# Projections of q, k and v in a hybrid decoder layer: seven half products per pair of column blocks, with the sums of the activations read back from DRAM

## The chip, the cores and the metric

One core of a Trainium2 chip runs the whole layer. The metric is the device time of one execution in microseconds; smaller is better. The engines are called by the profile's names: PE (matmul), PEld (its weight load), DVE (vector), ACT (scalar), POOL (GpSimd) and SP, which issues the DMAs.

## What is computed

The reference is one layer on 1024 tokens with 16 meta tokens ahead of them (L = 1040), width 1024, all in float32:

```python
xn = rms_norm(h, mix_pre_g[l])
proj = xn @ w_in[l]                      # z, xbc, dt, q, k, v
y_ssd = ssd_mixer(z, xbc, dt_raw, ...)   # Mamba-2 scan over chunks of 128
y_sb = rms_norm(stick_breaking_attention(q, k, v)..., sb_norm_g[l])
mix = jnp.concatenate([y_ssd, y_sb], axis=-1) @ w_out[l]
h = h + rms_norm(mix, mix_post_g[l])
xn = rms_norm(h, ffn_pre_g[l])
gu = xn @ w_up[l]
g = causal_dwconv(gu[..., :D_FF], ffn_conv_w[l], ffn_conv_b[l])
f = (jax.nn.gelu(g, approximate=True) * gu[..., D_FF:]) @ w_down[l]
h = h + rms_norm(f, ffn_post_g[l])
```

Stick-breaking attention weights a key by a sigmoid of q·k and by the product of (1 - sigmoid) over the keys between it and the query. q, k and v are 1024 wide each: 8 pairs of heads, 128 columns per pair of heads.

## The kernel before, in words

The normed input is transposed into `xs` (128 rows of one eighth of the width, 8 eighths, 1040 tokens) and split into a rounded part and the rest, so that a float32 product becomes three matmuls in the fast format: high·high, high·low, low·high. A projection block has 128 columns of a weight; `load_w` (L146 to L154) loads it (0.52 MB into the tag `wraw`, two buffers), ACT rounds it (`whi`), POOL takes the rest (`wlo`), three buffers each. `project_steps` (L156 to L168) then runs 8 eighths x 3 matmuls for each of three chunks of tokens (400, 384 and 256 wide, `CH`), each into one of two PSUM buffers `mm`; ACT copies a chunk out, and for k DVE takes the rest (L388, L389).

The order of the program: norm and transposes; projections for the SSD group (x, z, B, C); the scan of group 0 with the projections of group 1 between its chunks; the scan of group 1 with the first projections of q, k and v between its chunks; then the attention, a loop over 8 pairs of heads p and 8 query blocks i (from L989). One turn of that loop holds, on PE: the scores `z` of block i (L765), `av` of an earlier block (L802), one or two steps of the generator `fill`, which are the projections of the next pair of heads (half a chunk each, 12 matmuls), the transposes `tw` of an earlier block (L787), and another step of `fill`. PE's order is thus written out by hand; the orders of DVE, ACT, POOL and SP come from the scheduler of the framework, and each engine works its list in order. SP issues every DMA, in its order too.

For one query block, ACT takes two sigmoids of z, DVE multiplies along the keys with a scan (L773), POOL multiplies weight and remainder (L775, L776), PE transposes, ACT copies. `split_q` (L737 to L743) rounds a q block on DVE (`qh`, L741) and takes the rest (`ql`, L742). After q, k and v of the last pair of heads, the output product of the SSD half (`ssd_half`) takes the place of `fill`. The FFN that follows (L1304) already uses a scheme of seven half products, with its x sums held in SBUF.

## Time and profile before

| | |
|---|---|
| runs of the kernel before | 1734.75 us median of 3 (1733.84 to 1738.6) |
| the profiled execution | 1735.83 us, its span 1733.7 us |
| granted PE clock, mean | 0.995 |
| q, k, v projections on PE | from 310.4 to 820.1 us, between other work |
| attention, first scores of p = 0 | 400.5 us |
| moved by DMA | 173.87 MB, mean 100 GB/s |

In a row of groups stand line, engine, operation, output<-inputs, shape and count, then busy time, mean ns of one, and the idle time ahead of them with what ended it. In a timeline row stand the start and the length in us; matmul lengths are pipelined, so the distance of two starts is what one costs. In a row of windows stand the busy time of each engine in that stretch, the granted clock, the mean share of the 16 DMA engines in use, and GB/s.

### The profile page before, as it was taken

To read this page: it belongs to the slowest core of one execution; us is meant where nothing else is said; L and a number is where in the kernel's file an instruction comes from. 1 tells how busy PE (TensorE), PEld (TensorE's weight loads), DVE (VectorE), ACT (ScalarE), POOL (GpSimd) and SP (SyncE) were. 2 spreads that over 40 slices of the span, in tenths; PEclk is the share of its full clock that TensorE was granted. 3 is DMA by queue.
4 is the path that set the end of the run, shared out by engine and by line. 5 is a ranking of instruction groups with operands and counts; after the bars stand their busy time and mean duration, and the time that the engine had idled before them with its cause. 6 is when DMAs were issued, how large, how long until landed. Compare 5 with 4: busy or idle time off the path is not lost. (4 is left out here: it accounts for less than half of the span.)

```text
span 1733.7 us, 28039 instructions
## 1 busy us (share of the span) xinstructions
PE 1708.7 (99%) x11230; PEld 1498.9 (86%) x11230; DVE 1114.4 (64%) x1230; ACT 821.6 (47%) x1370; POOL 858.3 (50%) x645
## 2 busy tenths in 40 slices
PE   7999999999999999999999999999999999999998
PEld 6999889888999998998687778999988888887886
DVE  5752964775676686668531457676666666758777
ACT  5423653545566566567553245433333333343544
POOL 4323663685566576555642124587766777400001
PEclk9999999999999999999999999999999999999999
DMA  4232343231011111112215544233332222395335
GB/s 163 58 113 97 101 130 104 67 104 38 26 38 37 38 31 33 38 50 86 82 50 172 175 165 136 63 117 96 110 100 92 92 91 92 114 330 188 104 112 180
DMA packets 90674, 173.87 MB, mean 100 GB/s; under 512 B 10704, under 2 KB 35816, under 8 KB 90544
## 3 DMA queue, kind: packets, MB, share of 16 engines
q1 hardware_dynamic: 90544, 172.08, 31.0%
q8 instruction: 88, 1.44, 0.3%
q14 instruction: 42, 0.34, 0.1%
HBM read 122.32 MB, written 49.73 MB: 99 GB/s over the span
## 5 line engine op out<-in xcount | busy, mean ns | idle before, releaser
L775 POOL TENSOR_TENSOR bt<-bt,kp 128x256 f32<-128x256 f32 (+7 forms) x128 | 213.2, 1684 | 184.5 <-DVE kp L773 147.7
L773 DVE TENSOR_TENSOR_SCAN kp<-kp,hold 128x272 f32<-128x272 f32 (+7 forms) x128 | 183.4, 1473 | 26.0 <-ACT kp L766 14.1
L1247 POOL TENSOR_TENSOR wlo<-wr,whi 128x1024 fp32r<-128x1024 f32 x43 | 106.2, 2479 | 38.0 <-ACT whi L1246 38.0
L1751 POOL TENSOR_TENSOR fms<-fms 128x1 f32<-128x1 f32 x8 | 2.7, 333 | 223.7 <-DMA ar<-fda 187.5
L766 ACT ACTIVATE kp<-z 128x288 f32<-128x288 f32 (+6 forms) x112 | 82.5, 737 | 52.2 <-PE z L765 27.9
L1246 ACT ACTIVATE whi<-wr 128x1024 fp32r<-128x1024 f32 x43 | 45.6, 1059 | 111.5 <-PE fX L1304 68.3
L165 PE MATMUL pj_v<-xs,wh_v 128*128 128x400 f32 (+2 forms) x384 | 94.9, 334 | 0.0
L1376 DVE SCALAR_TENSOR_TENSOR ga<-gr,pp,ga 128x1024 f32<-128x1024 f32 x44 | 72.3, 1643 | 34.9 <-ACT ga L1369 34.1
L165 PE MATMUL pj_k<-xs,wh_k 128*128 128x400 f32 (+2 forms) x384 | 94.4, 333 | 0.0
L789 ACT ACTIVATE th<-tw 128x1024 f32<-128x1024 f32 (+2 forms) x96 | 75.6, 816 | 38.5 <-PE tw L787 38.4
L165 PE MATMUL pj_q<-xs,wh_q 128*128 128x386 f32 (+2 forms) x384 | 93.8, 331 | 0.0
L165 PE MATMUL pj_X<-xs,wh_X 128*128 128x400 f32 (+2 forms) x384 | 93.1, 330 | 0.0
L1636 ACT ACTIVATE dh<-ar 128x512 fp32r<-128x512 f32 x77 | 48.5, 630 | 92.4 <-PE dnB L1714 44.7
L165 PE MATMUL pj_z<-xs,wh_z 128*128 128x386 f32 (+2 forms) x384 | 91.5, 326 | 0.0
L741 DVE CAST qh<-q 128x128 fp32r<-128x128 f32 x64 | 46.9, 734 | 67.1 <-PE z L765 66.7
L1637 DVE TENSOR_TENSOR dl<-ar,dh 128x512 fp32r<-128x512 f32 x77 | 53.2, 691 | 50.3 <-ACT dh L1636 47.5
L951 PE MATMUL mo<-woa,yh 128*128 128x512 f32 x256 | 85.2, 400 | 0.0
L767 ACT ACTIVATE bt<-z 128x288 f32<-128x288 f32 (+6 forms) x112 | 82.8, 740 | 0.0
L802 PE MATMUL av<-th,v 128*64 128x128 f32 x1152 | 78.1, 280 | 0.0
L787 PE MATMUL tw<-ident,bt 128*128 128x128 f32 x576 | 75.4, 274 | 0.0
L802 PEld LDWEIGHTS av<-th,v 128*64 128x64 f32 x1152 | 62.3, 138 | 14.0 <-issue 11.3
L787 PEld LDWEIGHTS tw<-ident,bt 128*128 128x128 f32 x576 | 65.5, 141 | 5.8 <-issue 2.7
(560 smaller groups left out, 5635.2 us busy)
## 6 DMA issues: line engine op xcount, KB each, us to landing
wr<-in_w_up SPq DMA_DIRECT2D x44, 512.0 KB
fds<-ga SPq DMA_DIRECT2D x44, 256.0 KB
b<-in_w_down SPq DMA_DIRECT2D x44, 256.0 KB
ar<-fds SPq DMA_DIRECT2D x44, 256.0 KB
fda<-ga SPq DMA_DIRECT2D x33, 256.0 KB
ar<-fda SPq DMA_DIRECT2D x33, 256.0 KB
yk<-yd SPq DMA_DIRECT2D x16, 512.0 KB
wor<-in_w_out SPq DMA_DIRECT2D x12, 512.0 KB
```

The source lines that it names most:

```text
L165: mm(acc[:ncol, :n - s], a[:, k, :ncol], xs[c0][:, b, k, s:n], start=(k == 0 and j == 0), stop=(k == KB - 1 and j == 2))
L766: nc.scalar.activation(kp[:, :, a:a + w], z[:, :, :w], AF.Sigmoid, scale=-QSCALE)
L767: nc.scalar.activation(bt[:, :, a:a + w], z[:, :, :w], AF.Sigmoid, scale=QSCALE)
L773: nc.vector.tensor_tensor_scan(kp[:, j][:, ::-1], kp[:, j][:, ::-1], hold[:, L - n:L][:, ::-1], 0.0, op0=ALU.mult, op1=ALU.max)
L775: nc.gpsimd.tensor_tensor(bt[:, j, 0:m], bt[:, j, 0:m], kp[:, j, 1:m + 1], op=ALU.mult)
L787: nc.tensor.transpose(tw[:, j, b, :], bt[:, j, c0:c0 + P], ident)
L789: nc.scalar.activation(th[:, :, :nb, :], tw[:, :, :nb, :], AF.Copy)
L802: mm(av[halves[j], :], v[:, kb, halves[j]], th[:, j, b, :], start=kb == 0, stop=kb == i)
L951: mm(acc, u[:, k, :], v[:, cs], start=(k == 0 and j == 0), stop=(k == 7 and j == 2))
L1247: nc.gpsimd.tensor_tensor(l, raw, h.bitcast(F32), op=ALU.subtract)
L1376: nc.vector.scalar_tensor_tensor(v, self.g[jj][:, :, i:i + 256], fconv_w[:, j, i:i + 1], v, op0=ALU.mult, op1=ALU.add)
L1637: sub(lo[:, k], raw, hi[:, k].bitcast(F32), op=ALU.subtract)
```

## The change

Two blocks of 128 weight columns form a pair: (k, q), (v, q), (k, v), twelve pairs in all. The contraction is cut in two halves (4 eighths each) and the tokens in two halves of 520. Of the eight half products of such a 2 x 2 scheme, Winograd's form needs seven, on sums of weight quarters (s1 to s4) and of x quarters (t1 to t4). A half product is done in two steps of 260 tokens: 4 eighths x 3 matmuls = 12 matmuls each, so a pair has 14 steps. They run in the order 1 (x quarter b11), 2 (b21), 6 (t2), 5 (t1), 3 (b22), 7 (t3), 4 (t4).

- The x sums are formed once, during the scan of group 0: per eighth on POOL and DVE, rounded by ACT, and written to DRAM (`xt13`, `xt42`, 16 DMAs).
- For the steps with t1 to t4, the sums are read back into a ring of two slots, which takes the place of the quarter of x that no product uses by itself. A slot holds one step: 128 rows x 4 eighths x 520 float32 = 1.065 MB. When a step has used its slot, the DMA for the unit after next is issued into it. There are 96 units.
- DVE forms the weight sums (4 of 512 elements per pair). ACT rounds and POOL splits three and a half weight tiles per pair, where two blocks took two.
- The results of products 1 and 2 are copied out by ACT (k: ACT and DVE), those of 6, 5, 3, 7 and 4 are added by DVE from PSUM to what is in SBUF.
- `qh` is rounded by ACT and no longer by DVE.
- Chunks of the other projections are 320, 400 and 320 wide; a few constants move into the SSD pool, the scratch of dt into a buffer of `rkl`, which gets a third buffer; `FILL` goes, and `fill` is now run in steps of 12 matmuls throughout, 3 per turn for i < 3 and 2 for the others.

The core of the diff:

```diff
-CH = [(0, 400), (400, 384), (784, 256)]
+CH = [(0, 320), (320, 400), (720, 320)]
+HT = L // 2
+HP = HT // 2
+QKV = [(1, "a11", "b11", True), (2, "a12", "b21", False), (6, "s2", "t2", True), (5, "s1", "t1", True),
+       (3, "s4", "b22", False), (7, "s3", "t3", True), (4, "a22", "t4", False)]
...
+    def x_sums(k):
+        r1, r2 = (rp.tile([P, 2, HT], F32R, tag="rkl", name=f"xr{j}_{k}", bufs=3).bitcast(F32) for j in range(2))
+        for r, kk in ((r1, k), (r2, k + 4)):
+            nc.gpsimd.tensor_tensor(r, xq[:, kk, :, 0].bitcast(F32), xq[:, kk, :, 1].bitcast(F32), op=ALU.add)
+        nc.gpsimd.tensor_tensor(r1[:, 0], r1[:, 1], r1[:, 0], op=ALU.subtract)
+        nc.gpsimd.tensor_tensor(r1[:, 1], r2[:, 1], r1[:, 1], op=ALU.subtract)
+        nc.vector.tensor_tensor(r2[:, 1], r2[:, 1], r1[:, 0], op=ALU.subtract)
+        nc.vector.tensor_tensor(r2[:, 0], r2[:, 0], r2[:, 1], op=ALU.subtract)
...
+    ring = [xq[:, 0:4, 1].rearrange("p k b n -> p k (b n)")[:, :, 2 * HP * s:2 * HP * s + 2 * HP] for s in range(2)]
+    units = [(n, c) for _ in range(12) for n in ("t2", "t1", "t3", "t4") for c in range(2)]
...
+    def load_unit():
+        u = loaded[0]
+        if u < len(units):
+            loaded[0] += 1
+            (src, j), c = t_of[units[u][0]], units[u][1]
+            nc.sync.dma_start(out=ring[u % 2].bitcast(F32), in_=src[:, j, c].rearrange("p k b n -> p k (b n)"))
...
+        def split(self, raw, n1, n2):
+            hi, lo = self.slot(n1)
+            nc.scalar.activation(hi, raw, AF.Copy)
+            nc.gpsimd.tensor_tensor(lo, raw, hi.bitcast(F32), op=ALU.subtract)
...
+        def sums(self):
+            r1, r2 = self.r
+            nc.vector.tensor_tensor(r1[:, 0:4], r1[:, 0:4], r2[:, 0:4], op=ALU.subtract)
+            nc.vector.tensor_tensor(r2[:, 0:4], r2[:, 0:4], r2[:, 4:8], op=ALU.add)
...
+        def step(self, s):
+            (n, wn, xn, first), c = QKV[s // 2], s % 2
...
+            for k in range(4):
+                for j, (w, b) in enumerate(((hi, 0), (hi, 1), (lo, 0))):
+                    mm(acc[:, :HP], w[:, k, :], rv[:, k, b, :], start=first and k == 0 and j == 0,
+                       stop=k == 3 and j == 2, skip_group_check=not first)
+            if xn[0] == "t":
+                load_unit()
...
+            elif n == 6:
+                add(c21, a, c21, op=ALU.add)
+            elif n == 5:
+                add(c22, a, c21, op=ALU.add)
...
+    def qkv_flow():
+        post = []
+        for n, b in enumerate(blocks):
...
+            for s in range(14):
+                b.step(s)
...
+                if s == 0:
+                    b.split_s34()
+                if s == 2 and nxt:
+                    nxt.load(0)
+                if s == 3:
+                    b.split_s1()
+                if s == 5 and nxt:
+                    nxt.load(1)
+                    nxt.split_a()
+                if s == 8 and nxt:
+                    nxt.sums()
...
+                if s == 11 and nxt:
+                    nxt.split_s2()
...
-        nc.vector.tensor_copy(qh, q)
+        nc.scalar.activation(qh, q, AF.Copy)
...
-            run(fill, 1 + (i < FILL[p]))
+            run(fill, 1 + (i < 3))
...
-            run(fill, int((p > 0 or i > 3) and (p, i) != (6, 6)))
+            run(fill, 1)
```

How the change moves instructions is seen best at two places. The first is SP's list in the attention of p = 4. Before, the only large loads there are the weight blocks (`wr_q`, `wr_k`, `wr_v`), beside the store of an attention result (`yd`):

```order
L150 DMA wr_q_5690<-in_w_q 128x1024
L826 DMA yd_101<-ysc_4269 128x8x128
L150 DMA wr_k_5923<-in_w_k 128x1024
L433 DMA mvd<-v_5203 16x128
L150 DMA wr_v_6193<-in_w_v 128x1024
```

Now, about pairs 7 to 9 (`wr_8`, `wr_9` are the weights of pairs 8 and 9, `xall<-xt_109` the units of t1 and t3, `xall<-xt_110` those of t4 and t2):

```order
L385 DMA wr_8_6847<-in_w_k 128x1024
L966 DMA yd_92<-ysc_6127 128x8x128
L376 DMA xall<-xt_109 128x4x520
L385 DMA wr_8_6986<-in_w_v 128x1024
L376 DMA xall<-xt_109 128x4x520 x3
L376 DMA xall<-xt_110 128x4x520
L522 DMA mvd<-v_7177 16x128
L376 DMA xall<-xt_110 128x4x520 x3
L385 DMA wr_9_7460<-in_w_k 128x1024
L385 DMA wr_9_7570<-in_w_q 128x1024
L376 DMA xall<-xt_109 128x4x520 x4
```

Eight ring loads now stand between the first weight load of pair 8 and those of pair 9, and the loads of t1 of pair 8 stand behind both weight loads of pair 9.

The second place is PE's list in pair 4, where product 6 (t2) ends and product 5 (t1) begins. Before, the same place in the attention (block i = 3 of a pair of heads, scores `z_3`) reads x from SBUF only:

```order
L787 MATMUL tw_0_0_4895<-ident,bt_0_4645 128x128 x2
L165 MATMUL pj_v_0_4900<-xs_133,wh_v_4740 128x400 x2
L165 MATMUL pj_v_0_4900<-xs_133,wl_v_4741 128x400
...
L811 MATMUL twc_4913<-ident,cb_4068 128x128 x2
L765 MATMUL z_3_0_4921<-kh_3782,qh_3_4854 128x264 x2
...
L802 MATMUL av_0_4948<-th_0_0_4898,v_4495 64x128 x2
L822 MATMUL avc_4953<-thc_4916,vc_3894 64x256 x2
L165 MATMUL pj_v_0_4900<-xs_133,wh_v_4740 128x400 x2
```

Now (`pj_4_0` and `pj_4_1` are the two steps of pair 4's product; `whis_4_5012` is the weight sum s2, so those are the steps with t2, and `whis_4_5230` is s1, so those are the steps with t1):

```order
L464 MATMUL pj_4_0_5272<-xall,wlos_4_5013 128x260
L464 MATMUL pj_4_1_5287<-xall,whis_4_5012 128x260 x2
...
L927 MATMUL tw_0_0_5308<-ident,bt_0_5029 128x128 x2
L464 MATMUL pj_4_0_5313<-xall,whis_4_5230 128x260 x2
...
L951 MATMUL twc_5328<-ident,cb_4348 128x128 x2
L905 MATMUL z_3_0_5336<-kh_4176,qh_3_5245 128x264 x2
...
L942 MATMUL av_0_5363<-th_0_0_5311,v_4560 64x128 x2
L962 MATMUL avc_5368<-thc_5331,vc_3952 64x256 x2
L464 MATMUL pj_4_1_5374<-xall,whis_4_5230 128x260 x2
```

The first row is the end of the first t2 step. The load of the first t1 unit goes into the slot that this step frees, and the first t1 step (the row after `tw`) needs it: between them stand one step and two transposes.

326 lines of the change are left out of this document (196 added, 130 removed).

## The prediction

> **What bounds the kernel now.** I begin with the span and the busy times on the page, then read the stretches of the attention, where the changed projections lie.
>
> ```profile
> span 1733.7 us, 28039 instructions
> PE 1708.7 (99%) x11230; PEld 1498.9 (86%) x11230; DVE 1114.4 (64%) x1230; ACT 821.6 (47%) x1370; POOL 858.3 (50%) x645
> PEclk9999999999999999999999999999999999999999
> ```
>
> PE is busy for 99% of the span at full clock, so a matmul taken away shortens the kernel, unless PE then waits. The windows of the attention say who could make it wait:
>
> ```profile
> core 0: us, PE busy (x) PEld busy (x) DVE busy (x) ACT busy (x) POOL busy (x), PEclk, DMA share, GB/s
> 500.00:560.00 60.00, 60.00 (x517) 54.37 (x516) 41.12 (x43) 37.46 (x64) 36.38 (x28) 1.00 0.13 36
> 560.00:620.00 60.00, 60.00 (x503) 54.68 (x501) 43.55 (x40) 35.47 (x62) 35.65 (x29) 1.00 0.13 36
> ```
>
> PE has no gap at all; DVE is at 70%, ACT and POOL at 60%, and the DMA engines are nearly free (0.13). The time is PE's work, and the question is what the change makes of it and which of the other four comes late.
>
> **PE's work.** One eighth of a projection chunk is three matmuls. The distance of the starts of two such triples is their price, for 400, 384, 256 and, from the FFN, 258 columns (13 matmuls between the last two rows):
>
> ```profile
> 205.79 0.53 PE L165 MATMUL pj_X<-xs,wh_X 128*128 128x400 f32 x2
> 206.34 0.53 PE L165 MATMUL pj_X<-xs,wh_X 128*128 128x400 f32 x2
> ...
> 212.35 0.51 PE L165 MATMUL pj_X<-xs,wh_X 128*128 128x384 f32 x2
> 212.87 0.51 PE L165 MATMUL pj_X<-xs,wh_X 128*128 128x384 f32 x2
> ...
> 200.09 0.40 PE L165 MATMUL pj_X<-xs,wh_X 128*128 128x256 f32 x2
> 200.45 0.40 PE L165 MATMUL pj_X<-xs,wh_X 128*128 128x256 f32 x2
> ```
>
> ```profile
> 1157.05 0.28 PE L1304 MATMUL fA<-b11l,whi 128*128 128x258 f32 x1
> 1158.61 0.28 PE L1304 MATMUL fA<-b11h,wlo 128*128 128x258 f32 x1
> ```
>
> That is 0.55, 0.52 and 0.36 us a triple, and 0.12 us a matmul of 258 columns. A block of k or v costs 8 x (0.55 + 0.52 + 0.36) = 11.4 us, one of q (386 columns first) 11.2; 24 blocks are 272 us. Afterwards there are 12 pairs x 14 steps x 4 triples = 672 triples of 260 columns at 0.363: 244 us. **PE saves 28 us.** The chunks of 320, 400 and 320 of the other projections hold as many columns as before: nothing.
>
> **The ring.** This is the new wait. A step with a t sum can start only when its 1.065 MB have landed, and the load can be issued only when the step two units earlier has freed the slot. What a load takes is shown by the first loads of the kernel, issued by SP and awaited by ACT, and by the stretch in which the DMA is busiest:
>
> ```profile
> 0.79 0.39 SPq L235 DMA_DIRECT2D xt<-in_meta  x1
> 1.24 0.41 SPq L235 DMA_DIRECT2D xt<-in_x  x1
> 1.70 0.42 SPq L143 DMA_DIRECT2D gpre<-in_rows  x1
> ```
>
> ```profile
> 2.88 1.05 ACT L263 ACTIVATE junk<-xt 16x1024 f32<-16x1024 f32 x1 [0.81 <-DMA xt<-in_meta]
> ...
> 5.02 1.06 ACT L263 ACTIVATE junk<-xt 128x1024 f32<-128x1024 f32 x1 [0.99 <-DMA xt<-in_x]
> ...
> 8.21 1.06 ACT L263 ACTIVATE junk<-xt 128x1024 f32<-128x1024 f32 x1 [2.04 <-DMA xt<-in_x]
> ```
>
> ```profile
> 1515.00:1560.00 45.00, 45.00 (x200) 37.23 (x199) 24.56 (x39) 20.26 (x36) 0.00 (x0) 1.00 0.95 328
> ```
>
> The 64 KB of meta, issued at 0.79, are there at 2.88: about 2.0 us are fixed. From 5.02 to 8.21 gpre and the next x block land, 1.05 MB in 3.2 us; the busiest stretch gives 328 GB/s at a share of 0.95, 345 at full. So a unit streams in 3.1 us and is there 5.1 us after its slot is free; two units issued one after the other are there after 5.1 and 8.2.
>
> Against this stands PE's work between the end of the first step of one t product and the steps of the next. Prices of the work between (distance of starts):
>
> ```profile
> 588.44 1.91 PE L787 MATMUL tw<-ident,bt 128*128 128x128 f32 x16
> 590.11 0.60 PE L165 MATMUL pj_k<-xs,wh_k 128*128 128x384 f32 x2
> ...
> 593.15 1.97 PE L802 MATMUL av<-th,v 128*64 128x128 f32 x32
> 595.05 0.62 PE L165 MATMUL pj_k<-xs,wh_k 128*128 128x384 f32 x2
> ```
>
> ```profile
> 599.21 0.40 PE L765 MATMUL z<-kh,qh 64*128 64x264 f32 x2
> ...
> 600.14 0.44 PE L802 MATMUL av<-th,v 128*64 128x128 f32 x4
> 600.41 0.60 PE L822 MATMUL avc<-thc,vc 128*64 128x256 f32 x4
> ```
>
> 16 transposes take 1.67 us, 32 matmuls of av 1.90, the six z matmuls of 264 columns 0.93, a step 1.45. In the place shown from PE's list (pair 4, t2 to t1) one step and two transposes, 1.45 + 0.3 = 1.8 us, stand ahead of the first t1 step, which needs 5.1: it waits 3.3. The second comes at 1.8 + 1.45 + 0.3 + 0.9 + 0.3 + 0.5 = 5.3, which with the wait is 8.6: no more. I priced all 47 passages from one t product to the next in this way. Those across products 1 and 2 or 3 have 7 to 20 us and wait once (1.6 us, pair 2). Of the 24 direct ones (t2 to t1, t3 to t4), where 2 to 4 steps and the attention work between come to 3.5 to 10 us, 17 wait, by 0.1 to 4.7 us, the worst in pair 2, where three steps follow each other. The sum is **32 us**. With 0.6 us more of fixed time it is 45; at 36 GB/s for a share of 0.13 (277 at full, 3.85 us a unit) 60; at 4.5 us for one and 7 for two, 17. I take 32.
>
> **The weight loads in SP's list.** Each pair loads two blocks of 0.52 MB, 1.5 us each at that rate, and from pair 3 on one or both stand ahead of the t1 loads. They wait until POOL has split the last weights in that buffer, and what stands behind them in SP's list waits along. Before, SP already waits there, with nothing urgent behind:
>
> ```profile
> SPq L150 <- POOL wl_v L152: 127.8, 7, 26.3
> ```
>
> ```profile
> L775 POOL TENSOR_TENSOR bt<-bt,kp 128x1024 f32<-128x1024 f32 x12 | 34.8, 2922 | 21.9 <-DVE kp L773 13.0 <-PE z L765 4.8 <-PE vtc L428 4.1
> ```
>
> The buffer of the second block is freed by the split that starts after step 3, one step ahead of the one that frees the ring slot. If POOL is prompt this costs nothing. If the split takes ACT 1.06 (1024 wide, as in the rows above) and POOL 2.44 (the row of `wl_v` below) behind one product of 2.92, it takes 6.4 in all, and less the 2.7 of a step with its share of attention (57.1 us below by 21 steps) 3.7 us, for some ten pairs: 37. I take 10, nearer to nothing, since most t1 loads then only queue behind 1.5 us of weights.
>
> **The engines.** One p takes 60.7 us now (score rows of two pairs of heads), and 1.5 pairs fall into it:
>
> ```profile
> 575.15 0.33 PE L765 MATMUL z<-kh,qh 64*128 64x144 f32 x2
> ...
> 635.81 0.34 PE L765 MATMUL z<-kh,qh 64*128 64x144 f32 x2
> ```
>
> ```profile
> L741 DVE CAST qh<-q 128x128 fp32r<-128x128 f32 x56 | 42.3, 754 | 56.4 <-PE z L765 56.1
> L389 DVE TENSOR_TENSOR kl<-pj_k,kh 128x256 fp32r<-128x256 f32 x7 | 2.9, 416 | 4.5 <-ACT kh L388 4.5
> L152 POOL TENSOR_TENSOR wl_v<-wr_v,wh_v 128x1024 fp32r<-128x1024 f32 x6 | 14.6, 2440 | 0.5 <-ACT wh_v L151 0.5
> L1641 DVE TENSOR_TENSOR b<-b,b 128x512 f32<-128x512 f32 x44 | 29.1, 685 | 0.0
> ```
>
> PE's share falls to 57.1 us. DVE, 43 us now, loses 8 casts (6.0), gains 15 additions from PSUM at 0.42 (6.3) and 6 weight sums at 0.69 (4.1): 47.5, or 83%. POOL gains 2.25 splits of 2.44 (5.5): 41, 72%. ACT gains 8 short casts and 2.25 roundings: about 69%. None becomes the bound by itself, but each step's PSUM buffer is needed two steps later, and now mostly DVE must empty it, between its scans. The nearest row is the FFN, which works like this: PE's idle time there is 3.3 us for DVE and 1.1 for POOL in 410 us.
>
> ```profile
>   DVE pu L1400: 3.3, 9
>   POOL wlo L1247: 1.1, 3
> ```
>
> With the scans between I take **8 us**; the ends are 0 (hidden in the ring's waits) and 40 (one us for every fourth step). The x sums put 8 additions of 1040 elements and 8 of 520 on POOL ahead of the attention, about 30 us at `wl_v`'s rate; POOL is idle for half of the span, and I price them at nothing behind PE's projections, at 8 us if a weight split comes late.
>
> DVE's price depends on POOL. The same `ql` takes 0.29 us or 1.99:
>
> ```profile
> 578.88 1.99 DVE L742 TENSOR_TENSOR ql<-q,qh 128x128 fp32r<-128x128 f32 x1
> ...
> 584.90 0.29 DVE L742 TENSOR_TENSOR ql<-q,qh 128x128 fp32r<-128x128 f32 x1
> ```
>
> The Trainium skill ("SBUF — State Buffer", Who interferes with whom) says that a DVE instruction with two SBUF inputs and a GpSimd instruction that reads SBUF block each other for a whole instruction, while one with a single SBUF input goes free. By it the additions from PSUM stay at 0.42, and the weight sums, two SBUF inputs each, are the part of this change that pays: held by 1.7 us each they would make DVE 57.7 us a p, as much as PE. The trace agrees as far as `ql` goes.
>
> **The sum.** 1735.8 - 28 + 32 + 10 + 8 = 1757.8 in the profiled execution, which lies 1.1 above the median: **1757 us**, 1.3% slower.
>
> **The rivals.**
> - *The ring is hidden, and the kernel is faster.* If a unit takes 4.5 us and two take 7, the waits are 17 us and the rest hides in them: 1735.8 - 28 + 17 = 1725, 1724 as a median. It decides at 28 us of waiting in all. For it: the DMA engines are 87% free in the attention. Against: no row here streams faster than 345 GB/s, and a cover of 1.8 us is too short for any load. Chance 0.2. The Trainium skill ("DMA: Bandwidth & Descriptors", Anatomy of one DMA) gives 2.0 us plus bytes at 436 GB/s, 4.4 us for a unit, and is the page for this rival; the trace agrees with its 2.0 and not with its rate.
> - *Gain and waits cancel.* 32 us of ring waits with all else inside them, less what PE's own small pauses add to the cover: within 5 us of 1735. Chance 0.13.
> - *SP and DVE make it far worse.* SP held by POOL (37) and DVE late (18): 1735.8 - 28 + 32 + 37 + 18 = 1795. For it: SP's waits on POOL above, and DVE at 83%. Against: while PE waits, they catch up. Chance 0.17.
> - *The half products don't save what they count.* If each of 168 steps starts 0.2 us late, 34 us are lost and the result is near 1780 with the ring. Against: a chunk's first triple at 590.11 is the usual one after transposes, and the program before has nearly as many starts. Chance 0.05.
>
> **How the numbers follow.** The forecast (1741 to 1780) has the remaining 0.45. The range leaves out the lower part of the first rival and the worst of the third: 1722 to 1797. Less than 0.3%, about 5 us, is what a measurement of this kernel can't tell from no change. Faster: 0.2. Same: 0.13. Slower: 0.67.
>
> **What would show it.** The triples of the new products should start 0.36 us apart. In the list of waits PE should wait for DMA into `xall` some 20 times, longest near 5 us, in the steps of t1 and t4 and not of t2 and t3; SP's waits for POOL should stand ahead of t1 loads. DVE should be over 80% busy from 400 us on. I am wrong if a unit lands in under 4.5 us, or if PE's longest waits are for DVE or POOL.

## The result, and the profile after

The changed kernel takes **1864.91 us** (median of 4 runs, 1854.08 to 1872.54) against 1734.89 us of the kernel before (4 runs, 1733.84 to 1738.6): a ratio of 1.074, 95% interval 1.068 to 1.080. The forecast was 1757, the range ended at 1797. The profiled execution took 1872.54 us.

The page of the changed kernel, its span, busy times and clock:

```profile
span 1870.8 us, 29199 instructions
PE 1734.4 (93%) x11518; PEld 1512.9 (81%) x11518; DVE 1219.8 (65%) x1360; ACT 853.2 (46%) x1460; POOL 959.2 (51%) x685
PEclk9989999998899999989989999999999999999999
```

PE is now idle for 136 us where it was idle for 25. And it is busy for 26 us *more*, although its matmuls should take 28 less: the clock row has eights where every digit was a nine. The windows of the three stages (ahead of the first q/k/v step; from there to the first matmul of the output product; the rest) say where. Before:

```profile
0.00:310.40 310.40, 299.73 (x1943) 280.34 (x1943) 182.95 (x203) 140.23 (x265) 133.21 (x119) 0.99 0.35 109
310.40:833.40 523.00, 519.34 (x4237) 462.42 (x4236) 369.44 (x406) 317.12 (x565) 328.72 (x270) 1.00 0.17 49
833.40:1733.70 900.30, 889.59 (x5056) 756.10 (x5054) 562.03 (x623) 364.25 (x541) 396.37 (x257) 0.99 0.39 127
```

After:

```profile
0.00:333.80 333.80, 306.91 (x1942) 285.23 (x1943) 212.70 (x226) 147.30 (x275) 170.05 (x135) 0.97 0.40 124
333.80:968.40 634.60, 537.12 (x4526) 471.60 (x4525) 441.75 (x519) 343.08 (x645) 397.16 (x298) 0.92 0.61 203
968.40:1870.80 902.40, 890.34 (x5055) 756.02 (x5053) 565.33 (x616) 362.79 (x541) 392.01 (x252) 0.99 0.38 127
```

The first column is the length; behind it stand the busy times of PE, PEld, DVE, ACT and POOL, the granted clock, the share of the DMA engines in use, and GB/s. The first stage lost 23.4 us, the second 111.6, the rest 2.1. In the second, idle time went from 3.7 to 97.5 us (+94); busy time went from 519.3 to 537.1 where 28 less were due (491.3), so 46 us more were worked off at a lower clock: -28 + 94 + 46 = 112.

The list of PE's waits (in total, times, longest):

```profile
PE pj L464 <- DMA xall<-xt: 59.7, 22, 7.6
...
PE tt_X L611 <- DVE xtk L607: 9.7, 4, 4.8
PE pj L464 <- DVE kl L443: 8.8, 5, 2.6
```

The ring is the longest row, as forecast, but twice as long; about 38 us in the second stage are waits for other engines, in many short rows; and the `tt_X` row lies ahead of the attention, where the forecast had nothing.

A passage of the ring as the forecast described it, from the timeline of SP and then of PE (start, length, and in brackets the idle time ahead):

```profile
608.38 2.05 SPq L376 DMA_DIRECT2D xall<-xt  x2
610.07 0.36 SPq L376 DMA_DIRECT2D xall<-xt  x1
...
613.41 0.51 PE L464 MATMUL pj<-xall,whis 128*128 128x260 f32 x2 [1.43 <-DMA xall<-xt]
613.88 0.40 PE L464 MATMUL pj<-xall,whis 128*128 128x260 f32 x2
614.24 0.41 PE L464 MATMUL pj<-xall,whis 128*128 128x260 f32 x2
...
618.55 0.79 PE L464 MATMUL pj<-xall,whis 128*128 128x260 f32 x2 [2.98 <-DMA xall<-xt]
619.35 0.64 PE L464 MATMUL pj<-xall,whis 128*128 128x260 f32 x2
620.00 0.64 PE L464 MATMUL pj<-xall,whis 128*128 128x260 f32 x2
```

The first row holds both issues, the second row the later of them alone. The first unit is used 5.03 us after its issue (5.1 was forecast). The second is issued 1.7 us later, when its own slot comes free, and is used 8.5 us after that, 10.2 after the first's issue. The 8.2 of the forecast was for two loads issued right behind each other, so these 10.2 are not a slower load: SP issued 0.52 MB of an attention result (`yd`) at 612.52, and from 613.4 to 618.5 the DMA engines moved 335 GB/s, near the forecast's full rate of 345. The new triples start 0.36 us apart at 613.88, as forecast. But after the wait of 2.98 us they start 0.65 us apart (619.35 to 620.00), on the same tiles: PE works at about half its rate. Stretches like this are the eights in the clock row, and no term of the sum.

### The profile page after: what moved, and what is told of

Its sections match the earlier page's. It is cut to its first block, busy times and chain, and to the rows that moved or that the text cites. A ratio compares the mean times of both kernels' runs of the same rounds, so it can differ in the third digit from the quotient of the medians.

```text
span 1870.8 us, 29199 instructions
## 1 busy us (share of the span) xinstructions
PE 1734.4 (93%) x11518; PEld 1512.9 (81%) x11518; DVE 1219.8 (65%) x1360; ACT 853.2 (46%) x1460; POOL 959.2 (51%) x685
## 5 line engine op out<-in xcount | busy, mean ns | idle before, releaser
L464 PE MATMUL pj<-xall,whis 128*128 128x260 f32 x960 | 206.6, 313 | 76.2 <-DMA xall<-xt 59.7
L913 DVE TENSOR_TENSOR_SCAN kp<-kp,hold 128x272 f32<-128x272 f32 (+7 forms) x128 | 201.1, 1611 | 91.2 <-ACT kp L906 72.0
L464 PEld LDWEIGHTS pj<-xall,whis 128*128 128x128 f32 x960 | 162.3, 207 | 94.4 <-issue 29.2
L464 PE MATMUL pj<-xall,wlos 128*128 128x260 f32 x480 | 144.7, 301 | 2.3 <-POOL wlos L393 2.3
L464 PEld LDWEIGHTS pj<-xall,wlos 128*128 128x128 f32 x480 | 99.5, 207 | 2.8 <-POOL wlos L393 2.8
L160 PE MATMUL pj_z<-xall,wh_z 128*128 128x306 f32 (+2 forms) x384 | 94.4, 333 | 0.0
L160 PE MATMUL pj_X<-xall,wh_X 128*128 128x320 f32 (+1 forms) x384 | 94.0, 330 | 0.0
L1766 ACT ACTIVATE dh<-ar 128x512 fp32r<-128x512 f32 x77 | 48.5, 630 | 94.3 <-PE dnB L1844 44.8
L1084 PE MATMUL mo<-xall,yh 128*128 128x512 f32 x256 | 85.7, 402 | 0.0
L393 POOL TENSOR_TENSOR wlos<-wr,whis 128x1024 fp32r<-128x1024 f32 x24 | 64.2, 2677 | 39.4 <-ACT whis L392 36.3
L464 PE MATMUL pj<-xall,whia 128*128 128x260 f32 x384 | 76.2, 297 | 3.0 <-DVE q L489 3.0
```

The source lines that it names most:

```text
L160: mm(acc[:ncol, :n - s], a[:, k, :ncol], x_cols(k, b, c0 + s, n - s), start=(k == 0 and j == 0), stop=(k == KB - 1 and j == 2))
L464: mm(acc[:, :HP], w[:, k, :], rv[:, k, b, :], start=first and k == 0 and j == 0, stop=k == 3 and j == 2, skip_group_check=not first)
L913: nc.vector.tensor_tensor_scan(kp[:, j][:, ::-1], kp[:, j][:, ::-1], hold[:, L - n:L][:, ::-1], 0.0, op0=ALU.mult, op1=ALU.max)
L1084: mm(acc, u[:, k, :], v[:, cs], start=(k == 0 and j == 0), stop=(k == 7 and j == 2))
```

## The experiments

Theory A: the ring's landing time, and in the first stage the x sums, make PE wait, and each longer wait costs a second time because PE's clock is halved after it. The rivals: DVE and POOL are the bound behind the ring, or SP's list is. Most experiments leave work out, to see what it costs. Medians are given with the ratio to the kernel before and its 95% interval; before is 1735 to 1736 us in all of them. "Ideal" is 1708: before less the 28 us of matmuls.

### The clock: e4_clock_gaps

A kernel of its own, bursts of 100 matmuls of 260 columns, and between two bursts a chain of ACT copies that PE waits for:

```python
acc = burst(100, gap(acc, sizes), f"g{g}_{r}")   # gap: a chain of ACT copies, its result the next burst's weights
```

> A kernel by itself, none of the layer is computed: bursts of 100 matmuls of 260 columns on PE, between them gaps in which PE waits for a chain of ACT copies, from about 0.7 to 8 us, four of each; no DMA and no POOL beside them. Then bursts of 12 to 36 matmuls with short gaps in a row, and gaps of about 5 us with 0 to 30 extra matmuls at their start. Theory A (idle PE loses its clock): after gaps under 1.5 us a matmul costs 0.12 us as in the changed kernel at 601 us; after most gaps above 3 us it costs 0.2 to 0.27 for some 3.4 us, as at 618 us. Extra matmuls that shorten the idle part below 2 us keep the clock. Rival (the slow matmuls at 618 us come from the ring's DMA or POOL beside them): 0.12 after every gap, granted clock 1.00.

The first matmuls of some bursts (the bracket gives the gap):

```profile
204.49 0.39 PE L79 MATMUL acc_g<-xx,hold 128*128 128x260 f32 x1 [1.62 <-ACT hold L87]
218.26 0.39 PE L79 MATMUL acc_g<-xx,hold 128*128 128x260 f32 x1 [1.62 <-ACT hold L87]
...
248.78 0.39 PE L79 MATMUL acc_g<-xx,hold 128*128 128x260 f32 x1 [2.29 <-ACT hold L87]
264.85 0.39 PE L79 MATMUL acc_g<-xx,hold 128*128 128x260 f32 x1 [2.29 <-ACT hold L87]
...
358.83 0.39 PE L79 MATMUL acc_g<-xx,hold 128*128 128x260 f32 x1 [3.37 <-ACT hold L87]
375.89 0.39 PE L79 MATMUL acc_g<-xx,hold 128*128 128x260 f32 x1 [3.37 <-ACT hold L87]
```

With gaps of 1.62 a burst and its gap take 13.77 us. With 0.67 more of gap they should take 14.4; they take 16.07. With 1.75 more, 15.5; they take 17.06. Some 1.6 us are lost per gap, in matmuls of the burst that start 0.22 us apart in place of 0.12. None of the 16 gaps of 0.43 to 1.62 us lost anything, 3 of the 4 of 2.29 us did, 2 of 4 of 2.71, and all 16 of 3.37 to 7.06. No DMA and no POOL ran beside them, so theory A holds for the clock and its rival (the ring's traffic) falls. In the trace's record of the clock every half-rate stretch between the first burst and the last lasts 3.413 us or twice that, on one grid. That is what the Trainium skill ("TensorE: Matmul & The Clock Gate", Part 1: The HAM clock gate) states: half rate by default, a free-running window of about 3.4 us, full rate after a busy one. The runs agree with the window and differ on the gap: the Trainium skill's page puts the loss after an idle window of about 3.4 us, and here gaps of 2.3 us already lose. Nor does the length alone decide: with 12 extra matmuls at the start of a gap PE stood idle for 3.47 us four times and lost nothing. Those bursts repeated every 17.03 us, nearly five windows, so all met the same phase of the grid, and the gaps with extra matmuls told little else.

By the same record PE is at half rate for 13.7 us before and for 129.7 us in the changed kernel (without a last stretch of 3 us at the very end of each).

### The ring: e1_ring_stays, e2_half_units, e11_half_slots

e1 reads only the first two units:

```diff
+            if u < 2:
                 nc.sync.dma_start(out=ring[u % 2].bitcast(F32),
                                   in_=src[:, j, c].rearrange("p k b n -> p k (b n)"))
```

> Leaves out 94 of the 96 reads of the ring: the t steps use whatever the two slots got at first, all else is done. Theory A (PE waits for the units, and a wait of some 2.5 us or more halves PE's clock for a few us after it): the 59.7 us of waits for DMA go, and with them roughly half of the 54 us lost at half clock; the waits for DVE, ACT and POOL (38 us) stay: about 1872 - 60 - 27 = 1785, granted clock about 0.98. Rival B (DVE and POOL are the bound, and the ring's waits only give them time): PE waits for DVE instead, total above 1830. Rival C (the ring loads in SP's list hold up the weight loads, and these make DVE and POOL late): the waits for DVE and POOL go as well, about 1750.

**1820.12 us**, 1.049 (1.046 to 1.052): 45 us below the changed kernel, between A's 1785 and B's 1830. The waits of PE:

```profile
PE pj L465 <- DVE q L481: 13.4, 6, 3.8
PE pj L465 <- DVE kl L444: 10.4, 8, 2.3
...
PE pj L465 <- POOL wlos L394: 9.8, 2, 6.4
```

Its second stage:

```profile
333.50:920.20 586.70, 518.82 (x4528) 456.45 (x4525) 438.33 (x519) 342.16 (x645) 401.39 (x298) 0.95 0.15 48
```

The 59.7 us of waits for DMA are gone, but idle time in the second stage falls by 30 only (97.5 to 67.9), since waits for DVE and POOL come out behind them; busy time falls by 18 as clock. The ring costs 45 us. A is right on the ring and misses that about half of its waits cover waits for other engines: B holds for the rest, though not by its number. C falls: the waits for DVE did not go, they grew.

e2 and e11 change the size of what is awaited. e2 loads half of each unit after the first two; e11 computes everything, with four slots of half a unit:

```diff
-            nc.sync.dma_start(out=ring[u % 2].bitcast(F32),
-                              in_=src[:, j, c].rearrange("p k b n -> p k (b n)"))
+            e = 2 * HP if u < 2 else HP
+            nc.sync.dma_start(out=ring[u % 2].bitcast(F32)[:, :, :e],
+                              in_=src[:, j, c].rearrange("p k b n -> p k (b n)")[:, :, :e])
```

```diff
-    def load_unit():
-        u = loaded[0]
+    def load_unit(h):
+        u = loaded[h]
...
-            nc.sync.dma_start(out=ring[u % 2].bitcast(F32),
-                              in_=src[:, j, c].rearrange("p k b n -> p k (b n)"))
+            nc.sync.dma_start(out=ring[u % 2][:, 2 * h:2 * h + 2].bitcast(F32),
+                              in_=src[:, j, c, 2 * h:2 * h + 2].rearrange("p k b n -> p k (b n)"))
...
+                if xn[0] == "t" and k % 2:
+                    load_unit(k // 2)
```

> Each ring load after the first two brings the rounded halves of the unit alone (0.53 MB in place of 1.065; the rest parts stay those of the first two units). Theory A, by size: one unit is there after 2.0 + 1.55 = 3.6 us and two after 5.1, in place of 5.0 and 10.2 as the changed kernel's trace has them at 608 us; the waits for DMA fall from 60 to 15 or less, near what the first experiment gives plus 10 to 20 us: about 1800. Rival (a unit is late because SP issues it late or because every load has a long fixed time): the waits stay above 40 us, total above 1845.

> The whole computation, as changed, with the ring in four slots of half a unit (2 eighths, 0.53 MB) in place of two of a whole one: a step frees its first half six matmuls earlier, and a half is there after 2.0 + 1.55 = 3.6 us in place of 5.0. Theory A (cover against landing time): PE's waits for DMA fall from 60 to about 30, total 20 to 30 below the changed kernel: about 1840. Rival (the units come late because weight loads stand ahead of them in SP's list, or the DMA engines are simply full): the waits stay at 45 or more and the total above 1855.

e2: **1835.5 us**, 1.058 (1.055 to 1.060), waits for DMA 32.3 us; e11: **1839.48 us**, 1.058 (1.055 to 1.061), waits for DMA:

```profile
PE pj L465 <- DMA xall<-xt: 35.8, 21, 6.1
```

e11 is where A put it. e2's total fits neither: 35 above A, 10 below its rival, and 32 us of waits remain where at most 15 were expected: half the bytes did not take away three quarters of the waits. Of e2's 32 us, 27 lie in the steps of t1, and there a load does not land as a lone one does. A half unit by itself is there 3.4 to 3.6 us after its issue; behind a weight load the t1 loads that PE waited for took 4.4 to 6.2. And some are issued late. The timelines of PE, POOL and SP in the changed kernel, ahead of the longest wait of all, show both:

```profile
794.17 0.28 PE L464 MATMUL pj<-xall,wlos 128*128 128x260 f32 x1
...
791.10 5.85 POOL L915 TENSOR_TENSOR bt<-bt,kp 128x1024 f32<-128x1024 f32 x2
...
797.25 2.51 POOL L393 TENSOR_TENSOR wlos<-wr,whis 128x1024 fp32r<-128x1024 f32 x1
...
799.79 0.34 SPq L385 DMA_DIRECT2D wr<-in_w_q  x1
800.23 0.92 SPq L376 DMA_DIRECT2D xall<-xt  x2
...
806.27 0.77 PE L464 MATMUL pj<-xall,whis 128*128 128x260 f32 x2 [7.55 <-DMA xall<-xt]
```

The step that frees the slot ends at 794.45. The load is issued at 800.23, 5.8 us later: ahead of it in SP's list stands the weight load, which waits for POOL's split (797.25 to 799.76), which stands behind two of POOL's products (5.85 us). This is the chain that the forecast's third rival named. Then it lands, behind the weights, some 6 us after its issue in place of 5.1. This was pair 9; in pair 6 the same chain holds the load for 1.8 us. In pair 10 it is held for 5.1 us too, but behind a load of a stored SSD result (`yk<-yd`, issued at 853.54) that waits for DVE to free its buffer, not behind POOL. In pairs 3, 4 and 6 to 10 a weight load is issued 0.4 to 0.8 us ahead of a t1 load that PE waits for (in pairs 7 and 10 the second one), and PE starts on that 6 to 8.3 us after its issue. In pair 8 that is the whole of it: weights issued at 743.08, the unit at 743.52, and PE starting at 751.86 after a wait of 4.79.

### The x sums: e3_sums_copied, and part of e13_repaired

e3 replaces the body of `x_sums`:

```diff
-            nc.gpsimd.tensor_tensor(r, xq[:, kk, :, 0].bitcast(F32), xq[:, kk, :, 1].bitcast(F32), op=ALU.add)
...
+                for th in range(2):
+                    nc.sync.dma_start(out=dst[:, th, :, k, j, :],
+                                      in_=xq[:, kk, th, j].bitcast(F32).rearrange("p (c n) -> p c n", n=HP))
```

> The x sums are not formed: 32 DMAs copy plain quarters of x into the two DRAM arrays, so POOL, DVE and ACT have none of that work; the ring and all else stay as changed. Theory A (the sums make DVE late in the stage ahead of the attention, PE waits 14 us for the transposes of x blocks there and runs on at half clock): the first q/k/v step starts near 311 us in place of 333.8, total about 1872 - 23 = 1849. Rival (that stage is late for its new chunks of 320, 400 and 320 columns, which straddle the two halves of x): the first step stays near 333, total near 1870.

**1842.55 us**, 1.062 (1.059 to 1.065), first step at 311.7 us: theory A. The price is 22 us. POOL's and DVE's timelines in the changed kernel show how it came, and then PE's:

```profile
111.95 2.51 POOL L354 TENSOR_TENSOR xr<-xall 128x1040 f32<-128x1040 f32 x1 [5.30 <-DMA xt<-xr]
...
120.06 1.28 POOL L356 TENSOR_TENSOR xr<-xr,xr 128x520 f32<-128x520 f32 x1
...
121.37 0.70 DVE L357 TENSOR_TENSOR xr<-xr,xr 128x520 f32<-128x520 f32 x1 [5.81 <-POOL xr L356]
...
123.88 0.27 DVE L607 COPY xtk<-tt_X 16x128 f32<-16x128 f32 x1
...
124.21 1.11 PE L611 MATMUL tt_X<-ident,xsT 128*128 128x128 f32 x4 [4.79 <-DVE xtk L607]
```

POOL first waits 5.30 us for the store of earlier sums, which frees the buffer it writes to. DVE then stands for 5.81 us at a sum whose input POOL has not finished. Behind the three sum instructions stands the copy that frees a PSUM buffer (where PE writes its results, and which it can use again only when they have been read), and PE waits 4.79 us for it. POOL was half idle, as the forecast said: the wait that PE sees comes through the place in DVE's list. e3 takes the work, the stores and the place away together, so it prices all three and not the place alone.

### The engines: e5 to e10, e12, e14 and e16

e5 has e1's and e3's edits together and is the ground of the others.

> The first and the third experiment together: 94 of 96 ring reads left out, and the x sums not formed (32 DMAs copy plain quarters). If the two costs lie in different stages and add, the time is 1820 - 22 = 1798, the first q/k/v step starts near 311 us, and the stage from there to the first output product takes some 585 us, 62 more than before: that is what the engines cost by themselves, and the ground for the next three. Rival (the x sums' lateness is made up for later): 1815 or more.

**1797.93 us**, 1.036 (1.034 to 1.038). 1864.9 - 44.8 - 22.4 = 1797.7: the ring and the x sums add. (The changed kernel's four runs spread over 18 us, so each price is good to several us; e1 less e5 is 22.2 and e3 less e5 44.6.) Its second stage:

```profile
312.20:893.90 581.70, 515.71 (x4528) 453.87 (x4526) 438.41 (x519) 342.41 (x645) 402.90 (x298) 0.96 0.16 49
```

With neither ring nor sums 90 us above the ideal are left, in that stage 62 more of idle time (66.0 against 3.7) and 24 more of busy time at half clock. The forecast had 8. One of its waits, in the first block of a new pair of heads, from DVE's and then PE's timeline:

```profile
604.06 0.69 DVE L393 TENSOR_TENSOR wr<-wr,wr 128x512 f32<-128x512 f32 x1 [3.87 <-POOL wloa L385]
...
607.07 4.53 DVE L905 TENSOR_TENSOR_SCAN kp<-kp,hold 128x1040 f32<-128x1040 f32 x2
611.51 0.40 DVE L472 TENSOR_TENSOR q<-pj,q 128x260 f32<-128x260 f32 x1
...
611.97 0.51 PE L456 MATMUL pj<-xall,whis 128*128 128x260 f32 x2 [3.06 <-DVE q L472]
```

The addition that PE waits for stands behind two scans of the longest query block, and these behind four weight sums and a wait for POOL. Laying DVE's timeline over PE's waits of over 0.4 us ahead of steps that DVE ended (22 waits, 34 us in e5), DVE is scanning in 12.1, busy with remainders (`ql`, `kl`) in 8.8 and with additions in 5.3, and idle in 1.6. Of the stage's 66 us of idle time some 40 are waits for DVE, 15 for ACT and 10 for POOL. Which part of that can be taken away?

**e6_wsums_late** and **e16_no_pool_wait** are about the wait for POOL:

```diff
-                if s == 8 and nxt:
-                    nxt.sums()
...
                 if s == 11 and nxt:
+                    nxt.sums()
                     nxt.split_s2()
```

```diff
-            nc.gpsimd.tensor_tensor(lo, raw, hi.bitcast(F32), op=ALU.subtract)
+            free = hi.bitcast(F32) if n1 == "a11" else raw
+            nc.gpsimd.tensor_tensor(lo, free, hi.bitcast(F32), op=ALU.subtract)
```

> As e5, and the two weight sums that stand after step 8 of the pair before stand after step 11. Theory D (DVE stops in its list: the sum writes over a tile that POOL has still to split, DVE waits 20 us for POOL in all, and the additions that empty PE's PSUM buffers queue behind): DVE's waits for POOL at that line go below 5 us, PE's waits for DVE in the steps fall by 10 to 20, total 15 to 30 below e5. Rival W (DVE has too much work between its scans, whoever it waits for): within 5 us of e5.

> As e5, but POOL takes the rest of the first block of each pair from the rounded block alone (the rest comes out as zero), so that DVE's weight sums may write over the loaded block without waiting for POOL; POOL's and DVE's work stay the same in number and size. e6 was meant to test this, but the lists of all engines came out as in e5, so that it only repeated e5. Theory D (the wait in DVE's list, 18.7 us in e5, is passed on to PE through the additions behind it): DVE's waits for POOL at that line go to zero, total 10 to 17 below e5, as much as e7 gained without the sums. Rival W (the sums' 43 us of work are the price): within 5 us of e5.

e6: **1796.51 us**, 1.036 (1.034 to 1.038). It tested nothing: the scheduler put every instruction of every engine where it stood in e5. It shows that e5 repeats. e16: **1802.36 us**, 1.037 (1.035 to 1.039), no gain; the wait for POOL is gone and the sums take 1395 ns each in place of 889 (L393 in e5, L394 in e16):

```profile
L393 DVE TENSOR_TENSOR wr<-wr,wr 128x512 f32<-128x512 f32 x12 | 10.7, 889 | 24.1 <-POOL wloa L385 18.7 <-DMA wr<-in_w_q 2.8 <-DMA wr<-in_w_v 2.6
```

```profile
L394 DVE TENSOR_TENSOR wr<-wr,wr 128x512 f32<-128x512 f32 x12 | 16.7, 1395 | 21.4 <-DMA wr<-in_w_q 7.8 <-DMA wr<-in_w_v 4.4 <-ACT whia L384 3.0
```

DVE still stands idle for 21.4 us ahead of the first sum (24.1 in e5), now mostly for the weights to land, and the sums are longer. So a quicker release by POOL bought nothing, and theory D falls as far as POOL goes; whether PE pays for the sums' work or for DVE standing still ahead of them, e16 can't tell.

**e7_wsums_out**, **e10_adds_out** and **e8_qh_dve** change DVE's work: no weight sums; no additions of products 6, 7 and 4; q blocks rounded by DVE again.

```diff
-            nc.vector.tensor_tensor(r1[:, 0:4], r1[:, 0:4], r2[:, 0:4], op=ALU.subtract)
-            nc.vector.tensor_tensor(r2[:, 0:4], r2[:, 0:4], r2[:, 4:8], op=ALU.add)
...
-            nc.vector.tensor_tensor(s2, r2[:, 4:8], r1[:, 0:4], op=ALU.subtract)
...
-            nc.vector.tensor_tensor(r1[:, 4:8], r1[:, 4:8], s2, op=ALU.subtract)
```

```diff
-            elif n == 6:
-                add(c21, a, c21, op=ALU.add)
...
-            elif n == 7:
-                add(c22, a, c22, op=ALU.add)
-            elif n == 4:
-                add(c21, a, c21, op=ALU.add)
```

```diff
-        nc.scalar.activation(qh, q, AF.Copy)
+        nc.vector.tensor_copy(qh, q)
```

> As e5, and no weight sums at all: the splits take the plain quarters in place of s1 to s4, so DVE has 36 us less work and never waits for POOL there; ACT and POOL do the same work as before. Theory D: about as e6 (the wait was the price, not the work). Rival W (the work is the price): 30 to 50 us below e5 and well below e6.

> As e5, without the additions of products 6, 7 and 4 (72 of the 120 additions from PSUM; their results are dropped): DVE has 30 us less, and PE's buffers of those products wait for nobody. Theory S (PE waits for DVE to empty PSUM): PE's waits for DVE in the steps fall from 35 to 15 us or less, total 20 to 40 below e5. Rival (DVE's additions are hidden and the waits come from POOL's splits and ACT): within 8 us of e5.

> As e5, and q blocks are rounded by DVE again, as before the change. The rows of before and after: 60 roundings cost DVE 43 us before; after the change they are gone, but the remainders ql next to them went from 40.7 to 65.7 us and the scans from 161 to 180. If DVE's time is the bound, undoing it costs 20 us or more. If what DVE got was given back by ql and the scans, which only changed their neighbours, the time stays within 6 us of e5.

e7: **1781.35 us**, 1.026 (1.025 to 1.028), 17 below e5. It takes away both the sums' some 43 us of work and the 24 us that DVE stands idle ahead of them; the gain is less than rival W's 30 to 50 and within what D gave e6 (15 to 30), so which of the two is the price stays open. e10: **1793.04 us**, 1.032 (1.031 to 1.034), 5 below, less than the rival's 8: theory S falls for these additions alone. e8: **1801.21 us**, 1.038 (1.036 to 1.039), not to be told from e5. The rows of before and after (second stage) show why that one is empty. Before:

```profile
L773 DVE TENSOR_TENSOR_SCAN kp<-kp,hold 128x144 f32<-128x144 f32 (+7 forms) x114 | 161.2, 1454 | 10.5 <-ACT kp L766 9.6 <-POOL cb L776 0.2
L741 DVE CAST qh<-q 128x128 fp32r<-128x128 f32 x60 | 43.3, 723 | 56.5 <-PE z L765 56.1
L742 DVE TENSOR_TENSOR ql<-q,qh 128x128 fp32r<-128x128 f32 x60 | 40.7, 679 | 1.8
```

After:

```profile
L913 DVE TENSOR_TENSOR_SCAN kp<-kp,hold 128x144 f32<-128x144 f32 (+7 forms) x116 | 180.2, 1593 | 62.1 <-ACT kp L906 55.6 <-POOL wlos L393 2.6 <-POOL bt L915 2.3
L882 DVE TENSOR_TENSOR ql<-q,qh 128x128 fp32r<-128x128 f32 x60 | 65.7, 1094 | 0.8 <-ACT qh L881 0.6
```

43.3 us of roundings went from DVE, and 25.0 came back in `ql` and 19.0 in the scans (some 16 of it like for like, since the second window holds two scans more). e8 bears this out: with its roundings (38.8 us) back on DVE, `ql` takes 41.2 us in place of e5's 63.3 and the scans 176.5 in place of 185.6.

**e9_fill_moved** and **e12_fill_late** move steps between the query blocks. The means of e5 hide that blocks differ:

```diff
-            run(fill, 1 + (i < 3))
+            run(fill, (2, 3, 3, 1, 1, 1, 1, 1)[i])      # e9; e12: (1, 1, 1, 2, 2, 2, 1, 1)
...
-            run(fill, 1)
+            run(fill, (1, 1, 1, 1, 1, 0, 0, 1)[i])      # e9; e12: 1 everywhere
```

> As e5, but the steps of q, k and v are spread otherwise over the eight query blocks of a pair of heads: 3, 4, 4, 2, 2, 1, 1, 2 for i = 0 to 7 in place of 3, 3, 3, 2, 2, 2, 2, 2 (19 in both). In e5 one pair of heads has DVE busy for 7.35 of 7.35 us in block 6 and POOL for 9.12 of 9.12 in block 4 or 5.86 of 5.86 in another, while DVE is at 3.5 of 8.5 in block 1. Theory F (DVE and POOL are full in some blocks, and the mean hides it): PE's idle time falls by 20 or more and with it the half-clock time, total 20 to 40 below e5. Rival S (each PSUM buffer has one step to be emptied wherever the step stands): within 6 us of e5.

> As e5, with the steps spread the other way: 2, 2, 2, 3, 3, 3, 2, 2 for i = 0 to 7 (19, as before). e9 took steps out of the late blocks and lost 20 us; its rows and those of e5 show PE idle above all in block 0 of the next pair of heads (12.3, 17.1 and 9.8 us long in e9, 11.2, 14.2 and 10.1 in e5), with DVE busy for most of it. Theory Q (DVE's scans of the long blocks 5 to 7 are its queue; PE runs ahead of it there, and waits in block 0 for additions that stand behind them): with more PE work in blocks 3 to 5 DVE keeps up, block 0 comes down to 8 or 9 us, total 15 to 35 below e5. Rival S (one step to empty a PSUM buffer is too short in any block): the waits move to blocks 3 to 5, total within 6 us of e5 or above it.

e9: **1817.71 us**, 1.047 (1.044 to 1.049): 20 *worse* than e5, where 20 to 40 better was expected. Theory F had the full blocks right and the remedy upside down. e12: **1789.07 us**, 1.030 (1.028 to 1.032): 9 below e5. A windows row of block 0 (the first 144 columns of a pair of heads), in the kernel before, in e5, and in e12:

```profile
635.81:644.56 8.75, 8.75 (x82) 8.33 (x81) 6.56 (x5) 4.04 (x10) 6.91 (x6) 1.00 0.01 2
```

```profile
605.17:619.40 14.23, 10.23 (x81) 9.28 (x80) 12.79 (x15) 3.41 (x9) 7.22 (x6) 0.88 0.00 0
```

```profile
677.80:684.33 6.53, 6.53 (x69) 6.14 (x68) 6.49 (x7) 4.45 (x8) 6.07 (x3) 1.00 0.00 1
```

(e12's block 0 holds a step less, 69 matmuls for 81.) In e5 block 0 takes 14.2 us with DVE busy in 12.8: the scans of blocks 5 to 7 have piled up on DVE while PE ran ahead. With more PE work in blocks 3 to 5, block 0 came down to between 6.5 and 7.2 us in four of the five pairs of heads from 540 us on (one stayed at 13.8). Theory Q holds for a tenth of the 90 us, less than the 15 to 35 expected; the waits that remain moved into the middle blocks, as rival S said.

**e14_dve_relieved** has the edits of e7, e10 and e12 on e5's ground:

> As e12 (no ring reads, no x sums, steps spread later), and without the weight sums (as e7) and without the additions of products 6, 7 and 4 (as e10): DVE has about 65 us less than in e5. Theory Q (everything that is left is DVE's one list: PE's buffers wait behind scans and remainders, and each cause taken out alone leaves the rest to fill its place): the stage from the first step to the output product takes some 520 us in place of 582, total 1730 to 1745. If the three gains of the experiments simply add (17 + 9 + 5), 1767. Rival (POOL's splits and ACT's copies are as late as DVE): 1770 or more, with PE waiting for POOL and ACT.

**1753.31 us**, 1.010 (1.008 to 1.012): 45 below e5 where the single gains (17, 5 and 9) add to 30, and 45 above the ideal. It lies between theory Q's 1745 and the 1767 of gains that simply add; the rival's 1770 falls. Its second stage:

```profile
311.50:846.10 534.60, 501.21 (x4527) 444.44 (x4525) 390.35 (x403) 341.79 (x643) 387.01 (x296) 0.98 0.17 53
```

So DVE's added instructions (their work and their waits) and the place of the steps are together half of the engines' price, and these parts stand in for each other: one alone taken out gives little. The other half, 30 us of idle time over the kernel before and 10 of clock in this stage, is spread over waits of PE for DVE (20), ACT (8) and POOL (4); whose price it is stays open. One rival was not tested: PE comes back to each of its two PSUM buffers after one step of 12 matmuls, where it was a chunk of 24 before, and no run gave a third buffer.

### Repairs: e13_repaired, e15_kept_warm

e13 computes everything, with e11's half slots, e12's spread and the x sums on POOL alone (`nc.vector` to `nc.gpsimd` in three lines of `x_sums`). e15 is e11 with

```diff
+            warm = 16 if s == 6 and self.n > 2 else 0
+            for k in range(warm):
+                mm(acc[:, :HP], hold[:, :P], hold[:, P:P + HP], start=k == 0, stop=k == warm - 1)
```

> The whole computation, with three repairs together: the four half slots of e11, the spread of e12, and the x sums and their remainders on POOL alone, so that DVE does not wait in its list for POOL ahead of the attention. If the three causes lie in different places, their gains add: 1865 - 25 (e11) - 15 (most of the 22 of e3; POOL takes longer) - 25 (the middle of what e12 is expected to give) = 1800. If the ring's waits and the engines' waits cover each other, 1815 to 1835. Below 1736 only if what is called engines here was mostly the ring and the sums after all.

> The whole computation of e11, and ahead of the first step of product 5 in pairs 3 to 11 PE runs 16 matmuls on a tile of zeros into the buffer that the step will overwrite: about 1.9 us of the wait for the ring (2.6 to 6.1 us in seven of these nine pairs of e11, none in two) is spent working. Theory C (the half-clock time follows PE's idle stretches): the time at half clock falls from 109 us to 90 or less though nothing else is sooner, and the total by 3 to 8 us, the two pairs without a wait losing 4. Rival (the clock falls for another reason, the ring's own traffic): half-clock time stays near 109 and the total rises by 4.

e13: **1830.18 us**, 1.055 (1.053 to 1.056): 35 of the 65 us that the causes would give if they lay in different places, and within the 1815 to 1835 expected if their waits cover each other. The sums on POOL gained nothing: the first step came at 338.7 us, since now ACT's list stands at a rounding whose input POOL has not ready:

```profile
PE tt_X L608 <- ACT xsT L602: 11.1, 3, 5.2
```

e15: **1838.09 us**, 1.059 (1.057 to 1.061), not to be told from e11. The time at half clock fell from 109 to 61 us in the trace's record, with the ring's traffic as it was: theory C holds for the clock. No time was won: the 144 extra matmuls are some 17 us of PE's work themselves, more than the 3 to 8 us of gain expected.

## Why the prediction was wrong

The sign was right, and so was the account of the ring as a wait of PE. The sum was not: 22 us forecast, 130 measured, and most of what is missing is not the ring. Term by term:

| term | forecast | measured | from |
|---|---|---|---|
| PE's matmuls | -28 | -28 (counted) | triples 0.36 us apart; the ideal that the rest is counted from |
| the ring, with SP's list | 32 + 10 | 45 | changed kernel less e1 |
| the engines | 8 (ends 0 and 40) | 90 | e5 less the ideal |
| the x sums | 0 | 22 | changed kernel less e3 |

-28 + 45 + 90 + 22 = 129. The table closes because the 90 is what is left over the ideal: e14 shows the half of it to be DVE's added instructions and the place of the steps, and the other half has no shown cause.

- **The engines: the step that failed.** "None becomes the bound by itself" rested on DVE at 83% of a pair of heads, a mean over eight blocks. The windows row of block 5 in the kernel before has DVE (the fourth figure) busy in 6.62 of 6.66 us:

```profile
612.04:618.70 6.66, 6.66 (x59) 6.07 (x58) 6.62 (x6) 4.67 (x7) 4.24 (x4) 1.00 0.19 71
```

  (In the neighbouring pairs of heads DVE is busy for 89 to 99% of its fullest block.) What was added there found little room, and e12 shows for a part of it that it came out as PE's wait in block 0 of the next pair of heads. The mean misled in the other direction too: in the changed kernel's second stage DVE was busy for 441.75 of 634.60 us, 70%, where over 80% was forecast, and PE waited for it all the same, because an instruction is late by what stands or waits ahead of it in the list, not by the engine's share. The price of 8 us was scaled from the FFN (3.3 us of waits in 410), where no scans stand in DVE's list. The count of DVE's work was good (additions at 0.42 us, weight sums at 0.71 to 0.95), but the roundings taken from DVE bought nothing: most of their 43 us came back in `ql` and the scans.
- **No term for the clock.** "A matmul taken away shortens the kernel, unless PE then waits" leaves out that a wait of over some 2 us is paid twice. Some 53 us (7 in the first stage, 46 in the second) are matmuls at half clock; they are part of the measured prices of the ring, the engines and the x sums.
- **The x sums.** "POOL is idle for half of the span" was true and beside the point: DVE waited for POOL in its list, and PE's buffer behind that. The case named at 8 us (a late weight split) was another one.
- **The ring: the mechanism right, the size partly by luck.** One unit landed in 5.03 us (5.1), 22 waits were counted (18 passages), the longest 7.6 (4.7), and 41 of the 60 us lie in the steps of t1. The waits came to 60 us where ring and SP's list were priced at 42, since in seven pairs a t1 load ran behind weights, 6 to 8.3 us from issue to PE's start, and since SP's list held one for over 5 us in pairs 9 and 10. That the price was still 45 is two errors against each other: the clock added to the waits (18 us of busy time went with them in e1), and about half of the idle time came back in e1 as waits for other engines.
- **The third rival**, SP and DVE far worse, had the right two causes and was given 0.17; its 1795 was still 70 us short. Its ring and SP come to 69 us where 45 were measured, its DVE to 18 where the engines cost 90, and it had no x sums and no clock.

By the Trainium skill's rule that the forecast weighed ("SBUF — State Buffer", Who interferes with whom) the weight sums, with two SBUF inputs each, would be held by POOL. The traces agree in direction: in e5, e16 and the changed kernel, sums that ran beside no POOL instruction took 0.67 to 0.70 us, and all that took 0.9 to 2.4 us ran beside one. The means are 0.85 in the changed kernel (L401), 0.89 in e5 and 1.40 in e16: 0.2 to 0.7 us over a sum by itself, where 1.7 was the forecast's condition for a DVE as busy as PE.

## What to carry to other kernels

Judge an engine's room in the block where it is fullest, not by its mean over a loop, and ask what stands ahead of a new instruction in its engine's list: a short addition behind two long scans is as late as the scans. When PE has no gap at all, price each new wait of over some 2 us with 1.6 us on top for the clock (e4's loss per gap, an estimate for another kernel). And take out causes together as well as one by one: here single ones gave 17, 9 and 5 us, and together 45.

## What the runs showed of the hardware

- PE falls to half rate after idle gaps that are shorter than its clock's window: 2.29 us sufficed in 3 of 4 cases, 1.62 us in none of 4; the loss is 1.3 to 2.8 us each time, and the half-rate stretches last 3.413 us or twice that, on one grid. Where the gap lies on the grid counts too: 3.47 us lost nothing in four cases of one phase (e4).
- Short matmuls on zeros in a wait hold the clock (half-rate time 109 to 61 us), but saved no time here (e15 against e11).
- Work taken from an engine can come back in its neighbours: 60 `ql` on DVE went from 679 to 1094 ns each when the roundings ahead of them moved to ACT, and took 688 when these were back on DVE (e8).
- Weight sums on DVE (512 elements, both inputs in SBUF) took 0.67 to 0.70 us beside no POOL instruction, and up to 2.4 beside one.
